# A hybrid attention encoder step: the MLP's norm factor moved around the MLP, block 0's gate moved behind its MLP, and two groups of loads moved

## The chip, the core and the metric

The kernel runs on one core of one Trainium2 chip. The metric is device time in microseconds (us), lower is better. A core has a matrix engine (TensorE, "PE" in the profile, with its weight loads as "PEld"), a vector engine (VectorE, "DVE"), a scalar engine (ScalarE, "ACT"), a general engine (GpSimd, "POOL"), and a queue that issues transfers (SyncE, "SP"). Each works through its own list of instructions in order, and waits on semaphores for the others.

## The reference, cut to what matters

One layer over 2048 prompt tokens and 32 sample tokens, width 1024:

```
a  = rmsnorm(x, g_attn)
z  = a @ w_in                      # q, k, v of two groups of heads, 512 columns each
oa = differential attention        # group A: 4 heads, two q/k maps of 64, v of 128, T5 bias, chunk-causal
ob = chunk-band attention          # group B: 8 heads of 64, own chunk and the 8 before
h  = x + concat(rmsnorm(oa, subln_g) * c, rmsnorm(ob, out_norm_b)) @ w_out
c  = rmsnorm(h, g_mlp)             # h * (mean(h*h) + eps)**-0.5 * g_mlp
h  = h + square(relu(c @ w_up)) @ w_down
h  = h + sigmoid(h @ w_ple_gate) * (p @ w_ple_proj)    # p: per-layer inputs, 256 wide
y  = rmsnorm(h, g_final)
```

The sample tokens attend to cached keys and values of 128 past tokens as well. New keys and values are outputs too.

## The kernel before, in words

**Arithmetic.** Every product of 32-bit numbers is made of three matmuls: each operand is split into a high part (rounded) and a low part (the rest), and high x high, high x low and low x high are added up in PSUM (`mm3`, L164). `split` (L146) makes the parts: ACT or DVE the high one, DVE or POOL the low one. `wunit` (L155) loads a 512 KB piece of weights (`wr`) and splits it into `wh` (ACT) and `wl` (POOL).

**Tiling.** Tokens are cut into blocks 0, 1, 2 of 512 and block 3 of 512 + 32. Blocks 0 and 1 form the first half, 2 and 3 the second (`HALVES`). Matmuls have up to 512 columns; those of block 3 are 272 wide.

**Stages**, as `run` (L1074) writes them: `consts` (identity, and the gains, L191); `prep` of blocks 0 and 1 (L297: load 128 tokens, square sum, rsqrt, transpose, multiply by the gain, split into aH and aL); the projection of group A for the first half; `lam`, `biases` and `prep_p` (L753: loads the per-layer inputs p, transposes them through the PSUM ring "tp", splits them into tiles of the rings "qh" and "ql", two buffers each, and stores them to DRAM as pS); attention A of the first half (`attn_a`); the projection of group B, block by block, with `prep` of blocks 2 and 3 woven in; attention B of the first half (`attn_b`, L648); `caches` (L446); the rest of the projections; attention B and A of the second half; then output projections (`outproj`, L819), MLPs, gates and finals. The MLP of block 0, the MLP of block 1 with gate and final of block 1 come first; then `outproj` of 2 and 3, gate of block 0 woven with a norm, and at last one MLP for blocks 2 and 3 together, with their gates and finals.

**Norm in front of the MLP.** `outproj` adds up the squares of h and stores h to DRAM (hS). `colnorm2` (L870) sums the squares over the partitions with a matmul by ones and makes r = (mean + eps)**-0.5. `cnorm` (L848) loads h again, multiplies by g_mlp and r (L859, DVE) and splits into cH and cL. `mlp` (L951) runs in chunks of 256 hidden columns: `mlp_up` (L895), then `mlp_down` (L919) of the chunk before, whose products DVE adds to h (L949).

**Order.** A scheduler of the tile framework puts the instructions of all engines in order when the kernel is built, from its own estimate of times and from the order of the program as priority; so stages mix. What it can't change are the rings: a tile of a pool and tag gets the next of its buffers in the order of the program, and waits until the use of that buffer before it is over. Projections and MLPs of the first half take their PSUM tiles from two buffers ("mm"), attention's transposes from two others ("tp"), weights from two buffers (wr) and three (wh, wl).

**Attention B** works on units, one head and one pair of 128-token tiles (`attn_b_pair`, L670): scores (L704, PE), adding the bias and taking the maximum (L707, DVE), exp (L712, ACT), division (L714, ACT), transposes (L719, PE), split into pH (L728, ACT) and pL (L729, DVE), and the product with v (L744, PE). The rings of pH and pL have one buffer.

Of the kernel before, what the change touches and what calls it, by code (L numbers as in the profile page):

```python
# [12 lines left out]
F32 = mybir.dt.float32  # L13
# [119 lines left out]
class Kern:  # L133
# [57 lines left out]
    def consts(self, cp):  # L191
        nc, a = self.nc, self.a
        self.ident = cp.tile([P, P], F32, name="ident")
        make_identity(nc, self.ident)
        ones = cp.tile([P, P], F32, name="ones")
        nc.gpsimd.memset(ones, 1.0)
        self.ones = cp.tile([P, P], F32R, name="ones_r")
        nc.vector.tensor_copy(self.ones, ones)

        def cols(name, ap, k):  # L200
# [82 lines left out]
    def scratch(self):  # L283
# [3 lines left out]
        self.vS = [self.dram([KC, D], F32, "vSa"), self.dram([KC, D], F32, "vSb")]  # L287
# [9 lines left out]
    def prep(self, b, acts, pp, mm, tag):  # L297
        nc = self.nc
        aH, aL = acts[b]
        for c0, n in toks(b):  # L300
            t0 = 512 * b + c0
            x = pp.tile([P, D], F32, tag="x", name="x")
            self.dma(x[:n], self.xsrc(t0, n))
            a32 = pp.tile([P, 8, P], F32, tag="a32", name="a32")
# [23 lines left out]
            self.split(aH[:, :, c0 : c0 + n], aL[:, :, c0 : c0 + n], a32[:, :, :n], "dve", "pool")  # L328
# [490 lines left out]
    def outproj(self, b, wk, oact, ps, acc):  # L819
# [5 lines left out]
        for d in range(8):  # L825
            wh, wl = self.wunit(W[:, P * d : P * d + P].rearrange("(k p) c -> p k c", p=P), [8, P])
            h = wk.tile([P, BLK], F32, tag="tmp", bufs=4, name="hd")[:, :n]
# [17 lines left out]
            self.dma(self.hS[:, d, t0 : t0 + n], h)  # L845
            yield

    def cnorm(self, b, wk, act, out):  # L848
        nc = self.nc
# [4 lines left out]
        r = wk.tile([P, BLK], F32, tag="r", bufs=2, name="rl")[:, :n]  # L854
        self.dma(r, self.rS[:, t0 : t0 + n])
# [9 lines left out]
    def colnorm(self, *args):  # L865
        out = []
        drain(self.colnorm2(*args, out))
        return out[0]
# [50 lines left out]
    def mlp_down(self, ch, nf, blocks, us, st, wk, mm):  # L919
# [3 lines left out]
        for dh in range(nf):  # L923
# [6 lines left out]
            for d in range(nd):  # L930
                dd = nd * dh + d
                for b in blocks:
                    h = st[b][0]
                    for s0, sn in SUBS[b]:
# [14 lines left out]
                        nc.vector.tensor_tensor(hv, hv, ps, op=ALU.add)  # L949

    def mlp(self, blocks, st, wk, up, mm, md):  # L951
        nf = 2
# [121 lines left out]
    def run(self):  # L1074
        tc, nc, a = self.tc, self.nc, self.a
        with ExitStack() as top:
# [30 lines left out]
            with ExitStack() as x:  # L1107
# [3 lines left out]
                self.prep_p(sg, wk, ps_t)  # L1111
# [25 lines left out]
            self.caches(sg, tp)  # L1137
            drain(self.proj((3,), 1, acts, sg, mm, tp))
# [12 lines left out]
            self.small = False  # L1151
            sq_ = ExitStack()
# [9 lines left out]
            wk = opened(sq_, "wk", 1)  # L1162
            fk = opened(sq_, "fk", 1)
            self.gfin(fk)
            acc, cn, st = {}, {}, {}
            def norms(b, act, ps):
                self.colnorm(acc[b][0], b, 1.0 / D, wk, ps, "mm", self.rS)
                yield
                yield from self.cnorm(b, wk, act, cn)

            acc = {b: [] for b in range(4)}
# [15 lines left out]
            for b in HALVES[0]:  # L1187
                if b == 1:
                    drain(self.cnorm(1, wk, actq, cn))
# [4 lines left out]
                if b == 0:  # L1194
                    next(m)
                    self.colnorm(acc[1][0], 1, 1.0 / D, wk, mm, "mm", self.rS)
# [7 lines left out]
            wk = opened(top, "wk4", 1)  # L1204
            fk = opened(top, "fk4", 1)
            self.gfin(fk)
# [3 lines left out]
            weave(self.outproj(2, wk, oa[2], md, acc[2]), self.oload(3, wk, act, oa), 1, 0, OW)  # L1210
            g = self.outproj(3, wk, oa[3], md, acc[3])
            next(g)
            self.colnorm(acc[2][0], 2, 1.0 / D, wk, mm, "mm", self.rS)
# [12 lines left out]
            drain(f)  # L1226
# [57 lines left out]
```

## Time and profile before

| what | value |
|---|---|
| time, median of 3 runs | 3315.77 us (3314.72 to 3323.53) |
| the profiled execution: its time | 3310.69 us |
| the profiled execution: its span | 3308.8 us |
| mean granted TensorE clock | 0.975 |
| ACT, DVE, POOL busy | 51%, 50%, 44% of the span |
| bytes read and written in HBM | 379.06 MB, 110.49 MB |

The profile is one execution. Its views used here are: the page (busy time of each engine, the span in 40 slices), a table of windows (busy time of each engine in chosen stretches, with the clock that the throttle granted), groups of instructions by line and shape (count, busy time, mean in ns, the idle time of the engine just before them and what ended it), waits (who waited for whom), the same for one tile, and the time line. L12 is line 12 of the kernel before. A matmul's record has its length with its latency; how fast matmuls follow each other is read from their starts.

### The profile page before, as it was taken

What the parts mean: (1) busy time and instruction counts of PE and PEld (TensorE: products, weight loads), DVE (VectorE), ACT (ScalarE), POOL (GpSimd) and SP (SyncE); (2) the same over time, 40 slices, a digit from 0 to 9 for tenths busy, and PEclk for the clock granted to TensorE, in tenths of its full rate; (3) what the DMA queues carried; (4) which work ended last, traced back from release to release, by engine and by line L of the source; (5) the groups of instructions that cost most, each with busy time, mean ns of one, the idle gap of its engine ahead of it and who ended that gap; (6) DMA issues with size and microseconds to landing.
All of it is one profiled execution on the core that took longest, in us unless ns stands there. A gap on an engine that the chain in (4) does not pass through costs nothing. (4 is left out here: it accounts for less than half of the span.)

```text
span 3308.8 us, 50118 instructions
## 1 busy us (share of the span) xinstructions
PE 3096.1 (94%) x17881; PEld 2710.5 (82%) x17881; DVE 1669.4 (50%) x3952; ACT 1698.4 (51%) x3717; POOL 1468.8 (44%) x1083
## 2 busy tenths in 40 slices
PE   6988989999989999999899999989889999999998
PEld 6877778889977888777777877877779999999987
DVE  6117777454555545476765656656442232223335
ACT  4226666566665766666665656654442222222245
POOL 4335654432334433444544444565753333333365
PEclk9999899999999999999999999999999999999999
DMA  7488777686788654545655345347631111111123
GB/s 232 159 252 244 205 217 205 204 247 195 215 235 215 180 145 134 155 132 138 200 136 136 112 132 144 116 146 226 178 105 52 45 46 50 46 45 45 53 86 101
DMA packets 519073, 488.93 MB, mean 148 GB/s; under 512 B 37884, under 2 KB 414016, under 8 KB 518824
## 3 DMA queue, kind: packets, MB, share of 16 engines
q1 hardware_dynamic: 518824, 485.73, 50.8%
q8 instruction: 142, 2.33, 0.3%
q14 instruction: 107, 0.88, 0.1%
HBM read 379.06 MB, written 110.49 MB: 148 GB/s over the span
## 5 line engine op out<-in xcount | busy, mean ns | idle before, releaser
L153 POOL TENSOR_TENSOR wl<-wr,wh 128x1024 fp32r<-128x1024 f32 x338 | 820.0, 2427 | 1026.3 <-ACT wh L149 983.4
L949 DVE TENSOR_TENSOR h<-h,dps 128x512 f32<-128x512 f32 (+1 forms) x640 | 373.1, 585 | 584.6 <-PE dps L170 572.2
L149 ACT ACTIVATE wh<-wr 128x1024 fp32r<-128x1024 f32 x338 | 356.9, 1056 | 563.9 <-PE dps L169 278.4
L168 PE MATMUL dps<-uh,wh 128*128 128x512 f32 (+1 forms) x1280 | 459.7, 359 | 22.0 <-DVE h L949 16.7
L168 PE MATMUL ups<-cH,wh 128*128 128x512 f32 (+1 forms) x1280 | 452.0, 353 | 8.2 <-ACT relu L914 8.0
L170 PE MATMUL dps<-uh,wl 128*128 128x512 f32 (+1 forms) x1280 | 451.7, 353 | 0.0
L169 PE MATMUL ups<-cL,wh 128*128 128x512 f32 (+1 forms) x1280 | 451.5, 353 | 0.0
L169 PE MATMUL dps<-ul,wh 128*128 128x512 f32 (+1 forms) x1280 | 451.4, 353 | 0.0
L170 PE MATMUL ups<-cH,wl 128*128 128x512 f32 (+1 forms) x1280 | 451.0, 352 | 0.0
L168 PEld LDWEIGHTS dps<-uh,wh 128*128 128x128 f32 x1280 | 242.8, 190 | 57.0 <-DVE h L949 22.8
L168 PEld LDWEIGHTS ups<-cH,wh 128*128 128x128 f32 x1280 | 241.4, 189 | 40.9 <-ACT relu L914 8.6
L170 PEld LDWEIGHTS dps<-uh,wl 128*128 128x128 f32 x1280 | 241.7, 189 | 33.0
L169 PEld LDWEIGHTS ups<-cL,wh 128*128 128x128 f32 x1280 | 241.9, 189 | 31.1 <-DVE cL L153 0.4
L170 PEld LDWEIGHTS ups<-cH,wl 128*128 128x128 f32 x1280 | 241.7, 189 | 30.1
L153 POOL TENSOR_TENSOR ul<-relu,uh 128x272 fp32r<-128x272 f32 (+1 forms) x160 | 174.9, 1093 | 205.2 <-ACT uh L149 203.8
L169 PEld LDWEIGHTS dps<-ul,wh 128*128 128x128 f32 x1280 | 242.4, 189 | 26.3
L168 PE MATMUL qps<-aH,wh 128*128 128x512 f32 (+1 forms) x640 | 231.5, 362 | 6.8 <-ACT wh L149 3.4
L545 PE MATMUL s<-ka,q 128*128 128x256 f32 (+4 forms) x784 | 192.7, 348 | 40.8 <-issue 15.7
L169 PE MATMUL qps<-aL,wh 128*128 128x512 f32 (+1 forms) x640 | 229.8, 359 | 0.0
L170 PE MATMUL qps<-aH,wl 128*128 128x512 f32 (+1 forms) x640 | 229.3, 358 | 0.0
L559 ACT ACTIVATE e<-s,nm 128x512 f32<-128x512 f32 (+3 forms) x256 | 155.1, 610 | 94.7 <-DVE nm L551 70.9
L545 PEld LDWEIGHTS s<-ka,q 128*128 128x128 f32 (+1 forms) x784 | 135.7, 195 | 66.4 <-issue 27.9
(217 smaller groups left out, 7056.9 us busy)
## 6 DMA issues: line engine op xcount, KB each, us to landing
wr<-w_up SPq DMA_DIRECT2D x96, 512.0 KB, 4.2
wr<-w_down SPq DMA_DIRECT2D x96, 512.0 KB, 3.7
wr<-w_in SPq DMA_DIRECT2D x74, 512.0 KB, 5.2
q<-qS SPq DMA_DIRECT2D x256, 128.0 KB, 4.3
v<-vSa SPq DMA_DIRECT2D x64, 512.0 KB, 3.8
ka<-kS SPq DMA_DIRECT2D x32, 512.0 KB, 7.9
wr<-w_out SPq DMA_DIRECT2D x32, 512.0 KB, 5.0
wr<-w_ple_gate SPq DMA_DIRECT2D x32, 512.0 KB, 4.4
```

The lines of the kernel that those rows point to most:

```text
L149: nc.scalar.activation(hi, raw, AF.Copy)
L153: eng.tensor_tensor(lo, raw, hi.bitcast(F32), op=ALU.subtract)
L168: nc.tensor.matmul(ps, lh, rh, start=start and i == 0, stop=False)
L169: nc.tensor.matmul(ps, lh, rl, start=False, stop=False)
L170: nc.tensor.matmul(ps, ll, rh, start=False, stop=stop and i == n - 1)
L545: nc.tensor.matmul(s, q[:, m, hl, P * qi : P * qi + nr], kt[:, m, k0 : k0 + n], start=hl == 0, stop=hl == 1)
L559: nc.scalar.activation(dst, src, AF.Exp, bias=nmx, accum_out=z[:nr, m, bi : bi + 1])
L949: nc.vector.tensor_tensor(hv, hv, ps, op=ALU.add)
```

## The change

1. `consts` is cut in two: the four gain vectors are now loaded by a new method `gains`, which `prep` of block 0 calls right after it has issued its first load of tokens. `prep` of the first half takes its PSUM tiles in turn from two rings (three and two buffers) instead of one of three. In `prep`, ACT makes aH instead of DVE.
2. `prep_p` no longer stands behind `biases`, but behind `caches`, in a pool of its own that takes the space of the pool that `prep` has left.
3. The norm is put around the MLP. With v = mean + eps, relu(g h @ w_up)**2 @ w_down is v times what the reference's MLP gives, as the factor v**-0.5 passes through relu and is squared. So the MLP works on g h without the factor (`split_g`: ACT and DVE read h and multiply by g); before the first `mlp_down` adds to it, h is multiplied by v (POOL); and in the last chunk, each finished piece of h is multiplied by 1/v (DVE). `msnorm` makes v and 1/v and passes them through DRAM (vS[2] and rS).
4. Gate and final of block 0 follow its MLP directly, as those of block 1 do. The store of block 0's h, its load and its gate in the second half are gone.
5. In the second half, h of blocks 2 and 3 stays on chip from `outproj` on; block 2 is split during its `outproj`, block 3 behind its own; `oload` of block 3 is begun before.

```diff
-    def prep(self, b, acts, pp, mm, tag):
+    def prep(self, b, acts, pp, mm, tag, first=None):
...
             self.dma(x[:n], self.xsrc(t0, n))
+            if first is not None:
+                first()
+                first = None
...
-            self.split(aH[:, :, c0 : c0 + n], aL[:, :, c0 : c0 + n], a32[:, :, :n], "dve", "pool")
+            self.split(aH[:, :, c0 : c0 + n], aL[:, :, c0 : c0 + n], a32[:, :, :n], "act", "pool")
...
+    def split_g(self, k, src, n, c):
+        nc = self.nc
+        g = self.g_mlp[:, k : k + 1]
+        hi, lo = c[0][:, k, :n], c[1][:, k, :n]
+        nc.scalar.activation(hi, src, AF.Copy, scale=g)
+        nc.vector.scalar_tensor_tensor(lo, src, g, hi.bitcast(F32), op0=ALU.mult, op1=ALU.subtract)
...
-            tmp = wk.tile([P, BLK], F32, tag="tmp", bufs=4, name="tmp")[:, :n]
-            self.dma(tmp, self.hS[:, k, t0 : t0 + n])
-            nc.vector.scalar_tensor_tensor(
-                tmp, tmp, self.g_mlp[:, k : k + 1], r, op0=ALU.mult, op1=ALU.mult
-            )
-            self.split(cH[:, k, :n], cL[:, k, :n], tmp, "act", "dve" if k % 2 else "pool")
+            if hfull is None:
+                tmp = wk.tile([P, BLK], F32, tag="tmp", bufs=4, name="tmp")[:, :n]
+                self.dma(tmp, self.hS[:, k, t0 : t0 + n])
+            else:
+                tmp = hfull[:, k, :n]
+            self.split_g(k, tmp, n, (cH, cL))
...
                         nc.vector.tensor_tensor(hv, hv, ps, op=ALU.add)
+                        if rt is not None:
+                            nc.vector.tensor_tensor(hv, hv, rt[b][:, s0 : s0 + sn], op=ALU.mult)
...
-            if prev is not None:
+            if prev is None:
+                vt = self.hscale(blocks, st, wk, self.vS[2], "vt")
+                for d in range(8):
+                    for b in blocks:
+                        hv = st[b][0][:, d, : BN[b]]
+                        nc.gpsimd.tensor_tensor(hv, hv, vt[b][:, : BN[b]], op=ALU.mult)
+            else:
                 self.mlp_down(ch - 1, nf, blocks, prev, st, wk, md)
             prev = us
-        self.mlp_down(ch, nf, blocks, prev, st, wk, md)
+        self.mlp_down(ch, nf, blocks, prev, st, wk, md, self.hscale(blocks, st, wk, self.rS, "rt"))
...
-                    drain(self.prep(b, acts, pp, ps_s, "s"))
+                    ring = Rings((ps_s, "s"), (ps_t, "tp"))
+                    drain(self.prep(b, acts, pp, ring, "s", (lambda: self.gains(cp)) if b == 0 else None))
...
-                self.prep_p(sg, wk, ps_t)
...
             self.caches(sg, tp)
+            with ExitStack() as x:
+                self.prep_p(sg, opened(x, "pn", 1), ps_t)
             drain(self.proj((3,), 1, acts, sg, mm, tp))
...
-                if b == 0:
-                    self.dma(self.hS[:, :, 512 * b : 512 * b + 512], h)
-            drain(self.gate(1, h, uq, actq, mm))
-            drain(self.final(1, h, uq, fk, mm))
+                drain(self.gate(b, h, uq, actq, mm))
+                drain(self.final(b, h, uq, fk, mm))
...
-            h = hload(hh, BLK, 0)
-            g = self.gate(0, h, up, act, md)
-            next(g)
-            self.colnorm(acc[3][0], 3, 1.0 / D, wk, mm, "mm", self.rS)
-            drain(g)
-            for b in HALVES[1]:
-                drain(self.cnorm(b, wk, act, cn))
-            f = self.final(0, h, up, fk, mm)
-            st = {b: (hload(hh, BLK, b),) + cn[b] for b in HALVES[1]}
+            drain(self.csplit(3, wk, act, cn, hb[3]))
+            st = {b: (hb[b],) + tuple(cn[b]) for b in HALVES[1]}
```

More of the change, by code (lines that the diff above doesn't have):

```diff
@@ L826, in outproj @@
             wh, wl = self.wunit(W[:, P * d : P * d + P].rearrange("(k p) c -> p k c", p=P), [8, P])
-            h = wk.tile([P, BLK], F32, tag="tmp", bufs=4, name="hd")[:, :n]
+            if hfull is None:
+                h = wk.tile([P, BLK], F32, tag="tmp", bufs=4, name="hd")[:, :n]
+            else:
+                h = hfull[:, d, :n]
             self.dma(h, self.xT[:, d, t0 : t0 + n])
@@ L853, in cnorm, with msnorm @@
         out[b] = (cH, cL)
[L854 to L855 removed]
         for k in range(8):
[L857 to L868 removed]
+            if hfull is None:
+                tmp = wk.tile([P, BLK], F32, tag="tmp", bufs=4, name="tmp")[:, :n]
[3 more added lines that the diff above has]
+            self.split_g(k, tmp, n, (cH, cL))
+            yield
+    def msnorm(self, sq, b, wk, ps):
+        nc = self.nc
+        n, t0 = BN[b], 512 * b
+        sh = wk.tile([P, BLK], F32R, tag="sh", bufs=1, name="msh")[:, :n]
+        sl = wk.tile([P, BLK], F32R, tag="sl", bufs=1, name="msl")[:, :n]
+        self.split(sh, sl, sq, "act", "dve")
+        r = wk.tile([P, BLK], F32, tag="r", bufs=2, name="mr")[:, :n]
+        w = wk.tile([P, BLK], F32, tag="tmp", bufs=4, name="mw")[:, :n]
+        for s0, sn in SUBS[b]:
+            ss = ps.tile([P, 512], F32, tag="mm", name="mss")[:, :sn]
+            nc.tensor.matmul(ss, self.ones, sh[:, s0 : s0 + sn], start=True, stop=False)
+            nc.tensor.matmul(ss, self.ones, sl[:, s0 : s0 + sn], start=False, stop=True)
+            v = sq[:, s0 : s0 + sn]
+            y = r[:, s0 : s0 + sn]
+            z = w[:, s0 : s0 + sn]
+            nc.scalar.activation(v, ss, AF.Copy, scale=1.0 / D, bias=EPS)
+            nc.scalar.activation(y, v, AF.Ln)
+            nc.scalar.activation(y, y, AF.Exp, scale=-1.0)
+            nc.vector.tensor_tensor(z, v, y, op=ALU.mult)
+            nc.vector.tensor_scalar(z, z, -1.0, 2.0, op0=ALU.mult, op1=ALU.add)
+            nc.vector.tensor_tensor(y, y, z, op=ALU.mult)
+        self.dma(self.vS[2][:, t0 : t0 + n], sq)
+        self.dma(self.rS[:, t0 : t0 + n], r)
     def colnorm2(self, sq, b, scale, wk, tp, tag, dst, out):
@@ L917, in mlp_up, with hscale, mlp_down @@
         return us
-    def mlp_down(self, ch, nf, blocks, us, st, wk, mm):
+    def hscale(self, blocks, st, wk, src, name):
+        out = {}
+        for b in blocks:
+            out[b] = wk.tile([P, BLK], F32, tag="r", bufs=2, name=name)
+            self.dma(out[b][:, : BN[b]], src[:, 512 * b : 512 * b + BN[b]])
+        return out
+    def mlp_down(self, ch, nf, blocks, us, st, wk, mm, rt=None):
         nc = self.nc
```

48 lines of the change are left out of this document (28 added, 20 removed).

## The prediction

> **What bounds the kernel now.** I read the page first: span, share of each engine, the clock row.
>
> ```profile
> span 3308.8 us, 50118 instructions
> ...
> PE 3096.1 (94%) x17881; PEld 2710.5 (82%) x17881; DVE 1669.4 (50%) x3952; ACT 1698.4 (51%) x3717; POOL 1468.8 (44%) x1083
> ...
> PEclk9999899999999999999999999999999999999999
> ```
>
> TensorE is busy for 94% of the span, every other engine for about half. Its queue holds 17,878 instructions before and after the change, of the same shapes (the norm of the MLP costs as many small matmuls in its new form). So the time is TensorE's fixed work plus what it loses: idle time, and time at half clock. Next I read the table of windows, cut at the stages. Columns: window, length, busy time (instructions) of PE, PEld, DVE, ACT, POOL, then granted clock, DMA share and GB/s.
>
> ```profile
> 0.00:75.00 75.00, 50.16 (x360) 46.80 (x360) 49.28 (x124) 34.16 (x86) 39.10 (x29) 0.98 0.76 233
> ...
> 186.00:249.00 63.00, 53.49 (x304) 44.26 (x304) 11.36 (x24) 15.79 (x27) 23.97 (x18) 0.89 0.94 283
> ...
> 592.00:850.00 258.00, 247.14 (x1838) 235.08 (x1837) 124.73 (x427) 159.75 (x362) 83.43 (x93) 0.98 0.74 218
> 850.00:1130.00 280.00, 259.48 (x1438) 222.33 (x1437) 158.58 (x454) 182.47 (x349) 107.52 (x80) 0.96 0.78 217
> 1130.00:1360.00 230.00, 227.49 (x1236) 194.30 (x1236) 107.46 (x367) 142.64 (x290) 88.78 (x57) 1.00 0.51 136
> 1360.00:2170.00 810.00, 759.46 (x3837) 636.00 (x3836) 528.63 (x1109) 505.56 (x1177) 377.74 (x271) 0.99 0.51 141
> 2170.00:2310.00 140.00, 126.46 (x633) 105.01 (x632) 75.02 (x108) 68.58 (x129) 87.14 (x58) 0.96 0.62 197
> 2310.00:2490.00 180.00, 161.80 (x924) 142.19 (x925) 88.08 (x122) 79.71 (x146) 112.17 (x65) 0.95 0.47 144
> 2490.00:3170.00 680.00, 680.00 (x4213) 617.03 (x4212) 197.60 (x372) 192.27 (x327) 231.21 (x151) 1.00 0.16 47
> ```
>
> I count as a stage's loss its idle time plus (1 - clock) x length. Start: 24.8 + 1.5. Per-layer inputs (186 to 249): 9.5 + 6.9 = 16. First half of attention B (592 to 850): 10.9 + 5.2 = 16. The stretch 850 to 2170, where attention shares the chip with projections and the MLP of blocks 0 and 1: 32 + 3 + 59 = 94. The passage into the last MLP (2170 to 2490): 19 + 27 = 46. That MLP loses nothing. The change can win only out of these losses, and it can add to them.
>
> **The change, part by part.** The sum is against the profiled execution: 3308.8 us of span, 3310.7 us in all, which is 5.1 us under the median of the three runs (3315.77).
>
> *1. Per-layer inputs behind the caches: what it takes away from the overlap.* This is the largest term. `prep_p` puts its transposes into the PSUM ring that the attentions' transposes use (tag tp, two buffers) and its hi/lo halves into the ring that q and k of every projection use (tags qh, ql, two buffers each). Rings are handed out in the order of the program. Standing after the caches, `prep_p` comes behind all transposes of the first half of attention B, and q and k of block 3's projection come behind `prep_p`. So these 384 matmuls can no longer run beside that half, and what follows them in the weight ring cannot either. The order of the changed program shows it: on TensorE, 690 instructions (places 3126 to 3816 of 17,878) are attention B and nothing else: four heads' pairs of blocks 0 and 1, and all 16 units (head and pair of tiles) of blocks 2 and 3. Then come the 34 transposes of `prep_p` together. In the kernel before, the same half is spread over some 1,500 instructions among 900 projection matmuls. What does such a unit cost alone? The groups by form, window 600 to 1370:
>
> ```profile
> L714 ACT ACTIVATE eb<-eb,stb 128x640 f32<-128x640 f32 x96 | 79.3, 826 | 20.7 <-DVE stb L713 20.4
> L712 ACT ACTIVATE eb<-eb,stb 128x640 f32<-128x640 f32 x96 | 79.3, 826 | 47.6 <-DVE stb L711 47.6
> L728 ACT ACTIVATE pHb<-tpb 128x512 fp32r<-128x512 f32 x104 | 61.7, 594 | 29.9 <-PE tpb L719 22.4 <-PE ob L744 5.5
> L728 ACT ACTIVATE pHb<-tpb 128x128 fp32r<-128x128 f32 x104 | 28.3, 272 | 2.0 <-PE tpb L719 1.0 <-PE ob L744 0.5
> L749 ACT ACTIVATE t<-ob 64x256 f32<-64x256 f32 x64 | 24.4, 382 | 34.5 <-PE ob L744 31.3 <-DMA wr<-w_in 1.9
> L712 ACT ACTIVATION_READ_ACCUMULATOR eb<-eb,stb 128x1 f32 x128 | 24.1, 188 | 0.0
> ```
> ```profile
> L707 DVE CUSTOM_DVE_ANT_0 eb<-sb,bb 128x320 f32<-128x320 f32 x192 | 86.3, 484 | 75.7 <-PE tpb L719 70.7 <-issue 3.3 <-POOL ql L153 1.4
> L729 DVE TENSOR_TENSOR pLb<-tpb,pHb 128x512 fp32r<-128x512 f32 x104 | 71.1, 683 | 15.5 <-ACT pHb L728 13.5 <-PE tpb L719 1.7
> L729 DVE TENSOR_TENSOR pLb<-tpb,pHb 128x128 fp32r<-128x128 f32 x104 | 28.8, 277 | 3.4 <-ACT pHb L728 3.2
> ```
>
> ACT, per full unit of two tiles: 2 x (826 + 188 + 826 + 594 + 272) + 382 = 5.8 us. DVE is a little below (2 x (2 x 484 + 683 + 277) = 3.9 us, and small operations). TensorE's own pace is in the time line, columns start and length:
>
> ```profile
> 1292.39 0.31 PE L704 MATMUL sb<-kbt,q 128*128 128x320 f32 x1
> 1292.54 0.28 PE L744 MATMUL ob<-pHb,vbt 128*128 128x256 f32 x1
> 1292.66 0.60 PE L704 MATMUL sb<-kbt,q 128*128 128x320 f32 x3
> ...
> 1294.43 0.86 PE L719 MATMUL tpb<-ident,eb 32*128 32x32 f32 x6
> ```
>
> A score matmul takes 0.15 us; the 12 matmuls with v stand between 1292.54 and 1294.43, less three scores, 1.45 us; a transpose about 0.11. A unit is 8 x 0.15 + 1.45 + 10 x 0.11 = 3.7 us of TensorE. Alone, it waits for ACT, and pH and pL have one buffer, so a unit's halves also wait for the matmuls of the unit before: I take 6.2 us a unit. A head's two units of blocks 0 and 1 have as many keys as one full unit, but four tiles: by the rows 594 and 272 a column costs 0.84 ns, so an exp or scaling has 0.29 us of fixed cost and a copy 0.17; two more tiles with an accumulator read each and a second t add 2.3 us, less two copies' 0.33: 7.7 us of ACT, 8.2 with the same waits, against about the same 3.7. Sum: 16 x 6.2 + 4 x 8.2 = 132 us for 20 x 3.7 = 74 us of work: **+58 us**. Lower end: no waits, and the accumulator reads hidden (5.4 and 7.0): +40. Upper end: TensorE at half clock needs 7.4 us a unit and 9.5: +82. Of the 16 us that 592 to 850 lose now, 10 go (0 to 16), because attention is out of the way of the projections: **-10**.
>
> *2. `prep_p` itself, in its new place.* Its transposes and stores as they run now (tile ppt, tile pS, waits of TensorE in 186 to 249):
>
> ```profile
>   DMA pS<-ppl: 15.1, 3
> ...
>   DMA pS<-pph: 9.7, 3
> ```
> ```profile
> DMA to landing us min/median/max: 2.6/5.5/8.4
> ```
> ```profile
> PE ppt L770 <- DMA pn<-p_prompt: 6.9, 1, 6.9
> ```
>
> Its 8 pairs of halves go through two buffers, so ACT and DVE wait for stores to land (24.8 us now). The third and fourth loads of p still wait for the transposes of the first two. Now projections fill that time; in the new order nothing stands between the 34 transposes, and behind them, in TensorE's queue, wait q and k, whose evictions on ACT and DVE need the same buffers and whose first matmuls already hold both PSUM buffers of the projections. Four rounds of 2 us of eviction, 0.7 to issue and a landing: 4 us (between 2.6 and 5.5, as the queues are emptier there) gives 27 us, less 4 us of transposes: **+20** (14 at a landing of 2.6, 29 at 5.5). The Trainium skill, "DMA: Bandwidth & Descriptors", gives a fixed 2.0 us and the bytes at 436 GB/s, so 2.6 us for 256 KB; by that this term would be +14, and the whole sum 6 us lower, 3344. The shortest landing in the row agrees with it, the median is twice as long.
>
> The old place is freed: of 16 us lost in 186 to 249, 6.9 are the wait above, and the half clock behind it goes too: **-12** (5 to 16).
>
> *3. Token tiles first.*
>
> ```profile
> 0.74 0.47 SPq L144 DMA_DIRECT2D g_attn_s<-g_attn  x1
> ...
> 3.05 1.38 SPq L144 DMA_DIRECT2D x<-x_prompt  x3
> ...
> 12.89 4.65 POOL L153 TENSOR_TENSOR wl<-wr,wh 128x1024 fp32r<-128x1024 f32 x2 [11.39 <-ACT rsy L178]
> 12.93 2.32 DVE L179 TENSOR_TENSOR rsv<-rsv,rsy 128x1 f32<-128x1 f32 x1 [0.70 <-ACT rsy L178]
> ```
>
> The first tile's load moves from 3.05 to 0.74, 2.3 us earlier; the four gain loads go behind it, so the second tile gains nothing. A one-column DVE operation took 2.32 us while POOL split weights, and the chain to the second tile's transposes hung on it; five PSUM buffers in place of three, and aH on ACT, loosen this. **-6** (0 to -10).
>
> *4. Norm around the MLP, gate and final of block 0 directly behind its MLP.* Two waits stand in the passage into the last MLP:
>
> ```profile
> PE ups L168 <- ACT relu L914: 8.0, 1, 8.0
> PE gps L168 <- ACT wh L149: 7.5, 1, 7.5
> ```
>
> Both go: block 0's gate is no longer there, and block 2's halves are split during its out projection. What is late next is block 3's split: its buffers come free with the last out-projection matmul, and its 8 pieces take 8 x 1.1 to 1.7 us on DVE (rows below), against 5.8 us of block 2's first 24 matmuls (0.15 x 512/320 each). Of 46 us I take **-20** (-10 to -35).
>
> ```profile
> L949 DVE TENSOR_TENSOR h<-h,dps 128x512 f32<-128x512 f32 x384 | 261.9, 683 | 535.9 <-PE dps L170 534.1
> L949 DVE TENSOR_TENSOR h<-h,dps 128x272 f32<-128x272 f32 x256 | 111.5, 438 | 48.6 <-PE dps L170 38.1 <-DMA h<-hS 2.8
> L153 DVE TENSOR_TENSOR cL<-tmp,cH 128x512 fp32r<-128x512 f32 x12 | 13.3, 1119 | 1.8 <-ACT cH L149 1.8
> L153 DVE TENSOR_TENSOR cL<-tmp,cH 128x544 fp32r<-128x544 f32 x4 | 6.7, 1723 | 0.7 <-ACT cH L149 0.7
> ```
>
> New are 40 multiplies by 1/v on DVE in the last chunk of each MLP. Such an operation takes between 0.68 (the row from PSUM) and 1.12 us (from two SBUF tiles). Per d of the last MLP, DVE then needs 0.68 + 2 x 0.44 for the adds and 1.7 or more for the multiplies, 3.3 us, against 18 matmuls of 680/4213 = 0.16 us, 2.9 us, so the gate behind starts late: +2 at each MLP of blocks 0 and 1, +2 at the last, **+6** (2 to 12). The 32 multiplies by v on POOL (1.3 to 1.4 us each) stand one chunk ahead of the adds, under 144 x 0.16 = 23 us of matmuls of the next chunk at the last MLP: nothing, or about 5 if they hold up weights queued behind them on POOL. Block 1's h waits for block 0's final (one buffer), and its split for block 0's gate: **+3** (0 to 10).
>
> *5. Later stages.* Attention ends about 1,000 TensorE places earlier, so part of block 1's MLP runs without it: **-4** (0 to -56, see the rivals).
>
> Sum: 58 - 10 + 20 - 12 - 6 - 20 + 6 + 3 - 4 = **+35 us**: 3345.7 against 3310.7, and about **3350 us** on the scale of the median.
>
> **The rivals.**
> *The head start is paid back (faster).* Place: 850 to 2170. If its 94 us of loss come from attention sharing ACT and DVE, three fifths of them go as attention is done sooner (-56 in place of -4): the sum is -17, which on the median's scale is 3299. It decides against me from 39 us paid back. For it: in the row 2490 to 3170, without attention, the loss is zero. Against it: the amount of attention left for this stretch is the same.
> *Half clock in the lonely stretch (slower still).* The nearest row of attention with little beside it:
>
> ```profile
> 300.00:372.00 72.00, 55.07 (x306) 49.15 (x305) 58.57 (x174) 44.26 (x137) 44.81 (x47) 0.79 0.81 212
> ```
>
> At that clock or lower TensorE's part of each unit grows to where it sets the pace: the upper end, +82, which gives 3374. The Trainium skill, "TensorE: Matmul & The Clock Gate", What's actually happening, says the clock halves only after an idle window of about 3.4 us; gaps inside a unit are 1 to 2 us, so by that rule the forecast's full clock stands. The row's 0.79, with 55 of 72 us busy, says that it can fall in such a mixture.
> *The reordering does little (no change).* If ACT and DVE pass units at the lower end (+40), `prep_p` costs 14 in its new place and the passage gives 30 for 20, the sum is +1: 3317.
>
> **How the numbers follow.** Forecast 0.60, paid back 0.15, half clock 0.13, little change 0.12. The forecast's terms at their ends give about 3325 to 3385; with the rivals the range is 3296 to 3388. A measurement of this kernel tells about 0.3%, 10 us. Slower: 0.58 + 0.13 + 0.01; same: 0.02 + 0.10 + 0.02; faster: 0.13 + 0.01: 0.72, 0.14, 0.14.
>
> **What would show it.** In the profile after: a stretch of about 130 us of attention B with TensorE busy some 60% and ACT over 75%, followed by some 25 us around ppt with hardly any work; 186 to 249 full; the waits of 8.0 and 7.5 gone; the last MLP at no loss. If TensorE is over 85% busy in the lonely stretch, the largest term is wrong, and with it the sign.

## The result and the profile after

The changed kernel takes **3435.88 us** (median of 4 runs, 3431.43 to 3442.85); the kernel before takes 3315.24 on the same chip. The ratio is **1.0367, 95% interval 1.0341 to 1.0393**, about 120 us slower. The forecast was +35, and the range ended at 3388: right in sign, wrong in size.

The page of the changed kernel, the rows that were shown of before (span, busy time, granted clock by slice):

```profile
span 3434.6 us, 50124 instructions
...
PE 3164.9 (92%) x17881; PEld 2730.6 (80%) x17881; DVE 1682.5 (49%) x3954; ACT 1719.2 (50%) x3734; POOL 1481.0 (43%) x1099
...
PEclk9999999788999999999999999999999999999999
```

The eighth to tenth slices (about 600 to 860 us) hold three low clocks in a row, with a 7 that no slice of before had. The table of windows, cut at the stages, says the same in microseconds (length, busy time and instructions of PE, PEld, DVE, ACT and POOL, clock, DMA share, GB/s). First the kernel before:

```profile
0.00:249.00 249.00, 212.54 (x1202) 182.58 (x1203) 80.73 (x171) 75.39 (x153) 101.51 (x71) 0.96 0.68 214
...
1360.00:2118.00 758.00, 711.04 (x3594) 596.17 (x3593) 488.26 (x1029) 469.04 (x1092) 351.02 (x253) 0.98 0.51 142
2118.00:2490.00 372.00, 336.67 (x1800) 287.02 (x1799) 203.47 (x308) 184.80 (x360) 226.02 (x140) 0.96 0.51 161
```

Then the changed kernel:

```profile
0.00:249.00 249.00, 212.01 (x1203) 183.36 (x1204) 84.74 (x217) 87.88 (x194) 99.44 (x73) 0.95 0.66 203
...
593.00:838.00 245.00, 181.57 (x1014) 149.30 (x1014) 124.97 (x491) 161.83 (x366) 30.25 (x53) 0.81 0.66 189
838.00:1319.00 481.00, 460.28 (x2889) 412.59 (x2889) 229.97 (x709) 283.81 (x583) 173.26 (x136) 0.97 0.69 199
1319.00:2165.00 846.00, 783.68 (x3898) 645.12 (x3897) 553.51 (x1140) 524.20 (x1225) 401.69 (x294) 0.97 0.48 134
2165.00:2522.00 357.00, 336.36 (x1502) 269.95 (x1501) 142.74 (x193) 142.42 (x214) 199.90 (x107) 0.98 0.38 118
```

Counted as in the prediction (idle time plus (1 - clock) x length): the first 249 us lose 49 for 46. Attention B alone, with `prep_p` behind it, loses **110** where 592 to 850 lost 16. The stretch of attention A with MLPs 0 and 1, now with gate 0 in it, loses 88 for 62. The passage into the last MLP loses 28 for 50. That is +3, +94, +26 and -22. All stages together come to about +102 of the 126 us by which the span grew: 57 us more idle time and some 45 by the clock. The other 24 are in TensorE's busy time, which grew by 69 us for the same number of instructions. A matmul's record holds its latency, so time in which matmuls follow each other more slowly can count as busy; that this is where the 24 us lie is argued, not shown.

### The profile page after: what moved, and what is told of

Its sections match the earlier page's. It is cut to its first block, busy times and chain, and to the rows that moved or that the text cites. A ratio compares the mean times of both kernels' runs of the same rounds, so it can differ in the third digit from the quotient of the medians.

```text
span 3434.6 us, 50124 instructions
## 1 busy us (share of the span) xinstructions
PE 3164.9 (92%) x17881; PEld 2730.6 (80%) x17881; DVE 1682.5 (49%) x3954; ACT 1719.2 (50%) x3734; POOL 1481.0 (43%) x1099
## 4 chain that ended last, share of the span: by engine, by line
PE 64%; DVE 9%; DMA 7%; ACT 4%; issue 3%; POOL 1%; SPq 1%; DVEq 0%; POOLq 0%; ACTq 0%
PE ups L168 6%; PE ups L169 6%; PE ups L170 6%; PE dps L168 6%; PE dps L170 6%; PE dps L169 6%; PE s L551 2%; PE ob L750 2%; PE gps L168 1%; PE qps L168 1%; PE qps L169 1%; PE qps L170 1%; PE sb L710 1%; PE tpb L725 1%; PE gps L169 1%
```

## The experiments

Each ratio is against the kernel before on the same chip, with its 95% interval. Microseconds are worked out from the ratio, with 3312 for the kernel before; by that the changed kernel stands at +122.

### 1. `prep_p` back behind the biases

```diff
                 self.biases(wk, ps_t)
+                self.prep_p(sg, wk, ps_t)
...
-            with ExitStack() as x:
-                self.prep_p(sg, opened(x, "pn", 1), ps_t)
```

> The changed kernel with prep_p back behind the biases, everything else as changed. Theory (rings): the stretch of attention B alone and prep_p behind it lose 119.5 us of TensorE in the changed kernel against 19.4 in the kernel before, because q and k of block 3 stand behind prep_p in the qh/ql ring and prep_p behind attention B in the tp ring; with prep_p gone from there about 100 us come back: 3436 - 100 = 3336 (3320 to 3355), and what is left over the kernel before, about 20, is the stretch 1750 to 2042. Rival (norm and gate): most of the slowdown is in the MLPs, where DVE and POOL got more to do; then prep_p is worth its forecast of 68 at the most and this run is 3368 or more. Rival (half clock): the lonely stretch is dear because of the granted clock of 0.70 to 0.87; it would go here as well, so this run doesn't tell it from the theory.

Measured: 1.0015 (1.0001 to 1.0028), +5 us. Undoing this one part takes away 117 of the 122 us. What is left of the change, parts 1 and 3 to 5, costs 5 us.

### 2. `prep_p` alone moved, in the kernel before

The same edit the other way round, with nothing else changed.

> The kernel before with prep_p alone moved behind the caches, in a pool of its own. Theory (rings): the lonely stretch appears as in the changed kernel and costs the same: 3315 + 100 = 3415 (3395 to 3430), with a few us less if the old place gains. Rival (norm and gate): at most the forecast's 58 - 10 + 20 - 12 = +56, 3371, and less if the stretch costs this much only together with the early gate. The head start of attention B paid back later would show as less than 90 here.

Measured: 1.0326 (1.0297 to 1.0355), **+108 us**. Seen from both sides, the move of `prep_p` is nearly the whole slowdown. The rival that put it into the MLPs falls.

### 3, 5 and 6. Opening the chain of two rings

```diff
-                hi = sg.tile([P, BLK], F32R, tag="qh", bufs=2, name="pph")
-                lo = sg.tile([P, BLK], F32R, tag="ql", bufs=2, name="ppl")
+                hi = wk.tile([P, BLK], F32R, tag="ph", bufs=2, name="pph")
+                lo = wk.tile([P, BLK], F32R, tag="pl", bufs=2, name="ppl")
...
-                    tp = ps.tile([P, 512], F32, tag="tp", name="ppt")
+                    tp = ps.tile([P, 512], F32, tag="mm", name="ppt")
```

(and `mm` given to `prep_p` for `ps_t`). Number 3 has both edits, 5 the first, 6 the second.

> The changed kernel, with prep_p in its new place, but with buffers that attention B and the projections don't hold: its transposes take their PSUM tiles from the projections' ring (mm), its halves lie in tiles of its own. The same instructions and the same transfers. Theory (rings): no lonely stretch, 3335 (3315 to 3360), about as with prep_p in its old place. Rival (the work itself): prep_p costs what it does in the new place because its loads, stores and rounds stand beside the busiest transfers; then most of the 100 us stays, 3400 or more. Rival (half clock): the clock falls because attention runs without projections, so it goes with the stretch.

> As the run with both rings of its own, but only the halves of prep_p lie in tiles of their own; its transposes still take the attentions' PSUM ring (tp). Theory (a chain of two rings): attention B holds up prep_p through tp, and prep_p holds up q and k through qh/ql; with either link open the stretch of attention B alone goes. Then this run is about the run with both open, 3340 (3320 to 3360). Rival (one ring does it all, tp): the transposes behind attention B are in TensorE's list ahead of the projections and hold them up themselves; then 3400 or more.

> The other half: the transposes of prep_p take the projections' PSUM ring (mm), its halves stay in the ring of q and k (qh/ql). Theory (a chain of two rings): prep_p no longer waits for attention B, so q and k wait for prep_p only: the lonely stretch goes, but the rounds of two buffers with a store in each hold q and k up, so it may be somewhat over the run with both open: 3345 (3325 to 3370). Rival (one ring does it all, qh/ql): the stores are what holds q and k up, and the lonely stretch is only what is left over for TensorE meanwhile; then 3400 or more.

Measured: 1.0085 (1.0061 to 1.0110), 1.0051 (1.0036 to 1.0066) and 1.0091 (1.0074 to 1.0108): +28, +17 and +30 us. Work and place are those of the changed kernel, yet opening either link takes away 92 to 105 of the 122 us. So it is a chain: attention B holds `prep_p` through tp, and `prep_p` holds q and k through qh/ql. Where the transposes go still matters somewhat. In numbers 3 and 6 the 34 of them run as a burst, at 566 to 604 and 570 to 607 us; in number 5 they come at 850 to 879 us, beside projections, and that run is the fastest of the three (its interval touches that of number 3 and lies below that of number 6). The window 549 to 624, first of number 3, then of number 5:

```profile
549.00:624.00 75.00, 53.03 (x316) 46.38 (x315) 33.99 (x101) 35.58 (x90) 19.93 (x28) 0.77 0.80 240
```
```profile
549.00:624.00 75.00, 67.12 (x489) 60.83 (x487) 32.90 (x114) 38.80 (x99) 28.28 (x37) 1.00 0.69 211
```

TensorE is idle for 22 us at a clock of 0.77 in the first, and for 8 us at full clock in the second.

### 10. Two buffers for pH and pL in attention B

```diff
-        pH = pool.tile([P, 6, 256], F32R, tag="pH", bufs=1, name="pHb")
+        pH = pool.tile([P, 6, 256], F32R, tag="pH", bufs=2, name="pHb")
```

(pL likewise), in the changed kernel.

> The changed kernel with two buffers in place of one for pH and pL in attention B, nothing else. It tells what sets the pace of the lonely stretch, which took 187 us for the 132 of the forecast, 7.7 us a full unit for 6.2. Theory (latency of the chain: in the trace a unit's transposes and splits wait for the products of the unit before; 6.4 us from unit to unit at the best): two buffers let units overlap, ACT's 5.8 us a unit becomes the pace, some 20 units win 1 to 1.5 us each: 3436 - 25 = 3411 (3395 to 3425). Rival (half clock, and ACT's queue held up by the loads of the norm woven in): nothing changes, 3430 to 3440.

Measured: 1.0345 (1.0330 to 1.0360) for the changed kernel's 1.0367: 7 us less, and the intervals overlap, so a gain isn't shown; the execution that was profiled has a span of 3437.9 us for 3434.6. ACT's list of the changed kernel in the stretch (start, length, operation, idle time before it); each `t<-ob` ends a unit:

```profile
695.19 0.38 ACT L755 ACTIVATE t<-ob 64x256 f32<-64x256 f32 x1
...
701.57 0.38 ACT L755 ACTIVATE t<-ob 64x256 f32<-64x256 f32 x1
```
```profile
708.01 0.38 ACT L755 ACTIVATE t<-ob 64x256 f32<-64x256 f32 x1
...
712.03 0.63 ACT L798 ACTIVATE sqacc<-oraw 128x512 f32<-128x512 f32 x1 [3.34 <-DMA oraw<-oT]
...
718.60 0.38 ACT L755 ACTIVATE t<-ob 64x256 f32<-64x256 f32 x1
```

and with two buffers:

```profile
739.39 0.38 ACT L755 ACTIVATE t<-ob 64x256 f32<-64x256 f32 x1
...
745.84 0.38 ACT L755 ACTIVATE t<-ob 64x256 f32<-64x256 f32 x1
...
753.30 0.38 ACT L755 ACTIVATE t<-ob 64x256 f32<-64x256 f32 x1
```

A unit takes 6.4 us at the best with one buffer and with two: the buffers don't set this best pace, and that part of the theory falls. In the changed kernel the unit from 708.01 to 718.60 takes 10.6 us: ACT, which works in order, stands before a norm's load (oraw) for 3.34 us of it. There are four such waits in the stretch, 10.6 us in sum. With two buffers these loads are issued only after 799 us, the units take 7.1 us on average for 7.7, and the last one ends at 780.0 in place of 793.4. The 15 intervals between the full units are 8.5 us shorter in sum, less than these waits took, and the profiled execution had lost that again by its end.

### 4, 9, 13 and 14. Gate 0, the norm, and what the norm's multiplies cost

Number 4 moves only gate and final of block 0, in the kernel before; the store and load of block 0's h and its gate in the second half go with it:

```diff
...
-            drain(self.gate(1, h, uq, actq, mm))
-            drain(self.final(1, h, uq, fk, mm))
+                drain(self.gate(b, h, uq, actq, mm))
+                drain(self.final(b, h, uq, fk, mm))
...
```

> The kernel before with gate and final of block 0 alone moved behind its MLP; the norm stays in front of the MLP, and the store and load of block 0's h fall away. Theory (gate 0 holds up MLP 1): the split of block 1 and its h wait for gate and final of block 0, at a time when attention A is still running: +37 in the stretch of MLPs 0 and 1, less about 12 in the passage into the last MLP, where the gate is gone: 3315 + 25 = 3340 (3325 to 3350). Rival (the norm's multiplies): the 37 us come from the multiplies by v and 1/v on POOL and DVE; then only the passage's gain is left: 3303 (3295 to 3315).

Number 9 puts only the norm around the MLP (`msnorm`, `split_g`, the multiplies by v and 1/v), gate 0 as before. Numbers 13 and 14 take the multiplies out of number 9, first those by 1/v, then those by v as well. So the MLP's part of the result is too large by v in number 13, and lacks the norm's factor altogether in number 14:

```diff
-                        if rt is not None:
-                            nc.vector.tensor_tensor(hv, hv, rt[b][:, s0 : s0 + sn], op=ALU.mult)
...
-                        nc.gpsimd.tensor_tensor(hv, hv, vt[b][:, : BN[b]], op=ALU.mult)
```

> The kernel before with the norm around the MLP alone: v and 1/v instead of the factor in front, the splits straight from h; gate and final of block 0, the stores of h and the order stay. Theory (norm and gate are tied): gate 0 in the second half filled the wait for the norm of block 3. With the gate there, the norm's new place takes away only what the gate didn't cover: of the 24 us lost in 2310 to 2490 about 10, and the multiplies cost a few: 3311 - 8 = 3303 (3292 to 3315). Rival (the multiplies are dear): 3317 or more. Rival (the norm's place is worth much by itself): the run with gate 0 alone, +49, and the one with everything but prep_p, +5, differ by 44 or more; if all of that is the norm's, this run is at 3267.

> The run with the norm alone (+22), without the 40 multiplies of h by 1/v on DVE behind the last chunk of each MLP; the MLP's result is left too large by v. Theory (DVE's multiplies make the gates behind each MLP start late): the three gates get their h earlier; of the 22 us about 15 go: 3334 - 15 = 3319 (3312 to 3325). The forecast priced these multiplies at 6: then 3328. Rival (the order of the stages moves by itself, whatever the norm needs): 3330 to 3337.

> The same, without the 32 multiplies of h by v on POOL as well: only the splits straight from h are left of the norm's new form, and the norm's factor is missing altogether. Theory (POOL's multiplies hold up the weights' low parts queued behind them on POOL, 8 x 1.3 us for one block): a further 5 to 8 us: 3313 (3305 to 3320). The forecast priced them at nothing to 5. Rival (the order of the stages): as the run without the multiplies by 1/v.

Measured: gate 0 alone 1.0153 (1.0134 to 1.0173), **+51**, above the expected +25; the norm alone 1.0069 (1.0054 to 1.0083), **+23**; without 1/v 1.0004 (0.9991 to 1.0017), +1; without both 0.9932 (0.9913 to 0.9950), **-22**, below its expected range. So number 9 is 22 us slower for the multiplies by 1/v and 24 for those by v, where the prediction had 6 and "nothing, or about 5". The scheduler orders each version anew, and how much of these 46 us is new order and not the multiplies isn't told apart. What the norm's new place takes away without them is 22. That this is near the forecast's -20 is chance: the forecast spoke of one passage with gate 0 gone, and here gate 0 still stands there.

One place where v costs is in number 9's list of POOL and TensorE's waits:

```profile
2373.30 11.92 POOL L995 TENSOR_TENSOR h<-h,vt 128x512 f32<-128x512 f32 x8 [0.46 <-DMA vt<-vSm]
2385.18 2.79 POOL L153 TENSOR_TENSOR wl<-wr,wh 128x1024 fp32r<-128x1024 f32 x1
```
```profile
PE gps L170 <- POOL wl L153: 7.6, 1, 7.6
PE gps L168 <- ACT wh L149: 5.1, 1, 5.1
```

The 8.0 us wait of before (`ups <- relu`) is gone. In its place stand 7.6 us for a weight's low part, which sits behind eight multiplies on POOL. The rest of the 24 us, and the way in which 1/v costs, no view here shows.

Gate 0 cost at two places. The window of its new place and the passage into the last MLP, in the kernel before and then in number 4:

```profile
1683.60:1748.70 65.10, 61.87 (x302) 51.38 (x301) 43.09 (x95) 43.25 (x100) 28.63 (x23) 0.97 0.56 141
2313.40:2441.80 128.40, 111.15 (x602) 96.41 (x602) 62.16 (x64) 60.20 (x97) 93.53 (x54) 0.93 0.48 142
```
```profile
1689.50:1770.30 80.80, 64.91 (x303) 51.87 (x302) 59.27 (x128) 56.58 (x143) 37.72 (x30) 0.85 0.60 164
2357.90:2500.10 142.20, 105.53 (x601) 91.88 (x600) 61.69 (x88) 50.03 (x85) 65.45 (x38) 0.84 0.61 193
```

About 300 matmuls at gate 0's new place lose 28 us, and as many at that place before lose 5. That this is because MLP 1 can't start beside the gate is argued, not shown: number 7, which was to try it, lost its time elsewhere. The second rows lose 59 for 26: without gate 0 there, nothing covers the norm of block 3. TensorE's waits in number 4, from 2358 to 2500 us:

```profile
PE ups L168 <- ACT cH L149: 14.9, 3, 13.6
PE css L880 <- ACT sh L149: 6.3, 1, 6.3
```

With the norm around the MLP and h kept on chip (number 1) the same passage, the second row below, loses 8. The first row is gate 0's place there:

```profile
1686.00:1772.90 86.90, 63.59 (x302) 50.08 (x301) 69.29 (x139) 57.62 (x150) 41.50 (x34) 0.84 0.57 158
2355.00:2453.00 98.00, 92.78 (x602) 86.06 (x602) 51.25 (x68) 46.47 (x78) 54.84 (x30) 0.97 0.35 107
```

The two edits belong together: alone they cost 51 and 23 us, and together, with h on chip, 25 (number 12 below) or 5 (number 1, which has part 1 as well), not the 74 of their sum.

### 15 and 16. v on DVE, and the norm around the last MLP alone

```diff
-                        nc.gpsimd.tensor_tensor(hv, hv, vt[b][:, : BN[b]], op=ALU.mult)
+                        nc.vector.tensor_tensor(hv, hv, vt[b][:, : BN[b]], op=ALU.mult)
```

Number 16 also keeps the old norm for blocks 0 and 1.

> The run with the norm alone (+22), with the 32 multiplies by v on DVE in place of POOL. Without the multiplies by 1/v 20 us go, and without those by v another 26. Theory (POOL's list is what makes v dear: the weights' low parts stand behind the multiplies): most of the 26 come back, as DVE is busy half the time: 3334 - 18 = 3316 (3306 to 3326). Rival (the additions to h wait for v, whichever engine multiplies): 3328 to 3337.

> The kernel before with the norm around the last MLP alone (blocks 2 and 3), multiplies by v on DVE; blocks 0 and 1 keep the factor in front. Theory (the new place pays only in the passage into the last MLP, 12 us where v costs nothing; the multiplies by 1/v cost some 5 at the end, v on DVE 2): 3312 - 12 + 7 = 3307 (3298 to 3313), the one version so far that may be faster than both kernels. Rival (v is dear on DVE as well): the passage wins nothing, 3314 to 3322.

Measured: 1.0084 (1.0071 to 1.0096) and 0.9993 (0.9984 to 1.0002): +28 and -2 us. Number 15 went as its rival said: the 7.6 us wait for wl goes, but TensorE's places 6,000 to 11,100 (MLPs 0 and 1 beside attention) take 1063.5 us for the 1050.7 of number 9. So to move v off POOL's list won nothing. Whether that is a wait for v or the new order of the stages stays open. Number 16 is the fastest version that leaves nothing out, and it can't be told from the kernel before.

### 7, 8, 11 and 12. Other arrangements

Number 7 (number 1 with h in two buffers, both gates behind MLP 1):

> The changed kernel with prep_p in its old place, and with both gates and finals of the first half behind MLP 1: h of blocks 0 and 1 lie in two buffers, so that split and h of block 1 wait for nothing of gate 0. Theory (gate 0 holds up MLP 1): the run with prep_p in its old place loses 33.6 us in the 87 us of final 0 and the start of MLP 1, where the kernel before loses 5.6; about 30 come back: 3317 - 30 = 3287 (3275 to 3302), faster than the kernel before. Rival (the loss moves): two gates and finals in a row, with nothing woven in, wait for their own sigmoid and norm chains and for the splits of h; then 3305 to 3320.

Measured: 1.1223 (1.1203 to 1.1242), **+405**. Neither theory saw it. The window 1133 to 1742 us:

```profile
1133.00:1742.00 609.00, 398.15 (x1804) 313.79 (x1802) 346.27 (x1024) 355.89 (x962) 61.26 (x107) 0.71 0.42 103
```

Attention runs alone here for 600 us. The first split of an MLP's hidden values (uh) starts at 1825.8 us, right after attention A's last product at 1821.5; in number 1 it starts at 1088.6. With 16 KB more per partition for h, the tiles of uh presumably lie in memory that attention A still holds; that cause is argued from these times, not tried by itself.

Number 8 (part 1 alone), number 11 (gate 0 between the output projections of blocks 2 and 3, the norm around the MLP) and number 12 (parts 3 to 5 alone):

> The kernel before with part 1 of the change alone: gains behind the first load of tokens, five PSUM buffers for prep of the first half, aH on ACT. Theory (something else sets the start): TensorE's first instruction comes 6 us earlier in the changed kernel (4.8 for 10.9 us), but its place 300 at 67.2 us in both, so nothing is won at the start: 3313, the before of the same chip (3303 to 3320). Rival (aH on ACT helps the stages of attention A): the run with prep_p in its old place is 18.6 us ahead of the kernel before at place 2,700, with the same stages up to there but for part 1; if that lasts, 3295 to 3303.

> The kernel before with the norm around the MLP, gate and final of block 0 between the output projections of blocks 2 and 3, and h of these two blocks kept on chip; prep_p and the start as before. Theory (gate 0 must stand where nothing waits for it and where no norm has to be covered): MLP 1 keeps its start, as before, and the passage into the last MLP loses some 15 us, as in the changed kernel, in place of 46: 3311 - 25 = 3286 (3275 to 3300), faster than both kernels. Rival (gate 0 is a loss wherever it stands: its own splits and the wait of block 3's h for final 0 come into the passage): 3305 to 3325.

> The changed kernel without its parts 1 and 2: norm, gate 0 and h on chip as changed, start and prep_p as before. If the parts add up, this is the run with prep_p in its old place less what the start cost alone (+14): 3317 - 14 = 3303 (3293 to 3313). If the start costs nothing in this company: 3312 to 3320.

Measured: 1.0043 (1.0025 to 1.0062), 1.0076 (1.0058 to 1.0095) and 1.0075 (1.0059 to 1.0091): +14, +25, +25 us; three forecasts missed, each on the slow side. Number 8 is 18.7 us ahead of the kernel before at TensorE's place 2,700, its 2,700th instruction (530.1 us for 548.8), and has lost it by place 7,500 (1358.7 us in both). The parts don't add up either: start +14 and parts 3 to 5 +25, but number 1, which has both, +5. The scheduler orders each kernel anew; from these sums I take it that this moves 10 to 20 us either way, but no run tries the order by itself. Which order would keep the lead stays open.

## Why the prediction was right in sign and wrong in size

The runs divide the miss. The move of `prep_p` was forecast at 58 - 10 + 20 - 12 = +56, and measured 108 (number 2) and 117 (number 1). The rest of the change was forecast at -6 - 20 + 6 + 3 = -17, and measured +5 (number 1); term 5's -4 belongs to neither.

*Term 1, attention B alone (forecast +58, and -10 for the overlap).* The place and the chain of rings were right. The price was not. The stretch and what follows it, in the changed kernel:

```profile
606.00:671.00 65.00, 52.24 (x260) 42.06 (x258) 36.34 (x155) 50.64 (x128) 12.91 (x19) 0.74 0.83 229
671.00:793.40 122.40, 90.00 (x483) 71.60 (x483) 67.30 (x271) 86.07 (x182) 6.14 (x19) 0.86 0.52 141
793.40:838.00 44.60, 27.48 (x184) 25.16 (x185) 14.32 (x34) 15.78 (x33) 8.39 (x8) 0.73 0.76 247
```

The stretch took 187 us for the forecast's 132, and loses 30 + 49 = **79** for 58, some 34 of it by the clock. Three sizes were wrong. First, there was more work in it: 20 units of 30 instructions are 600, not the 690 that the prediction counted. In the trace the last projection matmul stands at 617.5 us. After the unit that ends at 618.55, 11 more of the short units end (those of tokens 0 to 511, which the prediction calls pairs of blocks 0 and 1): five and a half heads, where the forecast had four. The lines show the end of that unit, of the last short one, and of the first and the last full one:

```profile
618.55 0.38 ACT L755 ACTIVATE t<-ob 64x256 f32<-64x256 f32 x1
...
671.10 0.38 ACT L755 ACTIVATE t<-ob 64x256 f32<-64x256 f32 x1
...
677.89 0.38 ACT L755 ACTIVATE t<-ob 64x256 f32<-64x256 f32 x1
...
793.41 0.38 ACT L755 ACTIVATE t<-ob 64x256 f32<-64x256 f32 x1
```

Second, such a head took 9.6 us (52.6 for five and a half) for 8.2. Third, the 16 full units took 7.7 on average (15 intervals) for 6.2, though 6.2 was nearly the 6.4 that an undisturbed unit takes: some stood behind the norm's loads on ACT, and several ran partly at half clock. In the forecast's own terms, time less 3.7 us of work a unit, the 176 us from 617.6 to 793.4 lose about 96 (an estimate: 176 - 21.5 x 3.7). With term 2's 29, the 16 us that 592 to 850 lost and that went altogether (forecast -10), and the 3 us more of the first 249, that makes 112, between the 108 and 117 of the runs. This mis-sized term is the step that failed: 20 units at 6.2 and 8.2 us and at full clock gave +58, and the stretch cost 79 to 96.

*The range.* The prediction says that its terms at their ends give about 3325 to 3385. That sum is wrong: at the upper ends they give 82 + 29 - 5 - 10 + 12 + 10 = +118, or 3434 on the median's scale. The measured 3436 lies just beyond that, and so far outside the range. That the two nearly agree is chance: the passage came out as forecast, and the stretch, the old place, the multiplies and gate 0 went to their upper ends or past them.

*Half clock.* The forecast kept full clock, and its rival had half clock all through, 3374. The measured 0.74 and 0.86 lie between. The longest single waits of TensorE's lists between 665 and 793 us were (in all, times, longest):

```profile
PEld tpb L725 <- issue: 11.8, 17, 3.3
...
PE tpb L725 <- DVE pLb L735: 6.3, 4, 3.1
```

The prediction cited the Trainium skill, "TensorE: Matmul & The Clock Gate", What's actually happening, for a clock that halves after some 3.4 us of idleness. By that rule this stretch would stand at full clock, and it doesn't: the measurement decides. A later section of the same page of the Trainium skill, A second HAM failure mode: psum-queue depth-cycling, says of another kernel that frequent short idle spells between groups of matmuls make the clock swing as well; that agrees with the rows. No run here changes the clock by itself.

*Term 2, `prep_p` in its new place (forecast +20).* Right in mechanism, somewhat dear in fact: the third row above loses **29** us. (The prediction's 27 less 4 is 23, not 20, and at its shortest landing the same sum gives 17, not 14.) ACT's and TensorE's waits from 790 to 838 us, and the time from issue to landing of the stores (tile pS):

```profile
ACT pph L779 <- DMA pS<-pph: 13.6, 4, 8.7
```
```profile
PE ppt L776 <- DVE ppl L780: 16.1, 7, 8.7
```
```profile
DMA to landing us min/median/max: 2.1/4.0/7.6
```

The median landing is the 4 us that was assumed, and the longest wait of ACT, 8.7, is the first round. The Trainium skill's "DMA: Bandwidth & Descriptors", Anatomy of one DMA, gave 2.6 us for such a store by a fit to transfers that GpSimd issues, while SyncE issues these; the shortest landing here lies below it, the median above.

*The old place (forecast -12).* Nothing won: the first 249 us lose 3 us more than before. Between 186 and 249 us TensorE waits 8.3 us for a load of q, where it waited 6.9 for a load of p:

```profile
PE s L551 <- DMA q<-qS: 8.3, 1, 8.3
```

*Term 3, token tiles first (forecast -6).* TensorE starts at 4.8 us in place of 10.9 and reaches place 300 at 67.2 for 67.3, so the early start is gone by then. Three one-column operations of DVE took over 2 us each beside POOL's split, where before there were two:

```profile
13.62 2.32 DVE L179 TENSOR_TENSOR rsv<-rsv,rsy 128x1 f32<-128x1 f32 x1 [0.58 <-ACT rsy L178]
15.98 2.27 DVE L180 TENSOR_TENSOR rsv<-rsv,rsy 128x1 f32<-128x1 f32 x1
18.28 0.15 DVE L181 TENSOR_SCALAR rsv<-rsv 128x1 f32<-128x1 f32 x1
18.46 2.08 DVE L182 TENSOR_TENSOR rsy<-rsy,rsv 128x1 f32<-128x1 f32 x1
```

*Term 4, the passage (forecast -20, +6, +3).* It was -22 in the windows, so right there. The multiplies were the second mis-sized term: 22 for 1/v and 24 for v, measured in the kernel before with the norm alone (numbers 9, 13 and 14). Gate 0 behind MLP 0 cost 23 to 32 where it stands (number 4: 28 - 5; number 1: 37 - 5, from 86.9 us with 63.59 busy at a clock of 0.84), not +3. That is the size of the +26 in the stretch 1319 to 2165; how much of it there is gate 0's and how much the multiplies' isn't told apart.

*The rivals.* The paid-back head start fell: 838 to 1319 loses 35 us, as much as 850 to 1360 before (33). The rival of little change fell with the 79 and 29 us, where it had 40 and 14. The half clock was right in direction: with 0.74 and 0.86 the clock fell in part, and the +82 that it forecast for term 1 lies between the 79 and the 96.

*The signs named in advance.* The waits of 8.0 and 7.5 us are gone, and the last MLP loses nothing (719.2 of 720 us busy at full clock, 2522 to 3242). The stretch of attention B came, longer than named, with TensorE 76% and ACT 73% busy. The window 186 to 249 is not full: 52.8 of 63 us busy, at a clock of 0.86.

## What to carry to other kernels

Before a step is moved, list the rings from which it takes buffers, and who comes before and behind it in each: two rings in a row turned a light step into a barrier of over 100 us, and another ring on either side took away all but 17 to 30 us. A piece of work that looks like a cost may be the cover of a wait: move it only together with the wait, and try what replaces the wait by a run that leaves it out: the multiplies, forecast at 6 to 11 us, came to 46 there. A shift won early is kept only if no later stage gives it back, so it is measured at the end of the kernel.

## What the runs showed of the hardware

TensorE's clock fell to 0.74 over 65 us and 0.86 over 122 us with no wait of its lists over 3.3 us in either stretch, and to 0.71 over the 609 us where attention ran alone (number 7). DVE's slow one-column operations above have two SBUF operands and run beside POOL's split; the one between them, with a single operand, took 0.15 us.
